# A mixture-of-experts layer on one core: a transposed wide form for experts over 128 tokens, longer weight pieces, and permuted features

## The chip, the cores and the metric

One program runs on one core of a Trainium2 chip. The metric is the device time of one execution in microseconds (us); lower is better. The core has TensorE (PE: matmuls, with weight loads shown apart as PEld), VectorE (DVE), ScalarE (ACT), GpSimd (POOL) and SyncE (SP, which only issues DMAs here), and 16 DMA engines behind the DMA queues.

## The reference, cut to what matters

The layer has a mixer (attention and a short convolution), a mixture of experts, and a gated per-layer embedding. The change touches the experts:

```
# 2048 tokens, D = 1024 features, hidden size FF = 512, 32 experts, 2 experts per token
xn = rmsnorm(h)                                # (2048, 1024) float32
group logits = xn @ w_group_router             # top group of 4
expert logits = xn @ w_expert_router           # top 2 of the 8 experts of that group
for every expert e, over the tokens routed to it:
    hidden = silu(x @ w_gate[e]) * (x @ w_up[e])    # (n, 1024) @ (1024, 512)
    y      = hidden @ w_down[e]                     # (n, 512) @ (512, 1024)
h += sum over a token's two experts of weight * y
```

With the inputs of the runs 16 of the 32 experts have more than 128 tokens (experts 0, 2, 8 to 11, 15 to 18, 20, 22, 25 to 27 and 31); the largest has 155.

## The kernel before, in words

**Precision by splitting.** Every float32 operand of a matmul is split into a high and a low part: ACT copies the tile to `uh` (the rounded value), DVE subtracts that to get `ul`. A product then takes three matmuls, `hi*hi`, `hi*lo` and `lo*hi`, added up in one PSUM bank; `mm3` issues them (L73, L74, L75, in the order uh·xh, ul·xh, uh·xl as the names of the trace have it).

**Weights.** Each expert has 12 units of 512 KB: four of `w_gate`, four of `w_up`, four of `w_down`. SP loads unit by unit into a ring of 12 raw slots (`load_unit`, `unit_loads`); `split_unit` turns a raw slot into a pair `uh`, `ul` in a ring of 10 (L65 on ACT, L66 on DVE); PE reads the pairs. `free()` in an expert's block splits the next unit into the pair just used up and issues the loads for which room is left. A partition's piece of a `w_gate` load is two rows of 2 KB, of a `w_up` load four rows of 1 KB, of a `w_down` load one row of 4 KB.

**Tokens.** POOL gathers the first 128 tokens of an expert into `xg0` (one token a partition) and, for an expert with more, up to 64 "others" into `xg1`; that second gather stands in an `If` of its own one expert ahead. PE transposes them (128x128 for the first, 64x64 for the others) and ACT and DVE split the results into `xh`, `xl` (features on partitions, 128 tokens) and `xs` (64 tokens, high and low side by side). What exceeds 192 tokens would go through another loop, `far_experts`; it has no work here.

**An expert's block.** The 32 experts are written out one after the other. Each is an `If` on its count: `block(e, True)` for over 128 tokens (called wide below), else `block(e, False)` (near). In both the tokens are the stationary operand and the weights move past them. Near: per unit of `w_gate` two times three matmuls of 512 columns, per unit of `w_up` four times three of 256, per unit of `w_down` two times three of 512. After the second and fourth `w_up` unit, DVE multiplies with the silu of the gate to get `u` (128 tokens x 256 hidden values, L1299), PE transposes it (L1306), ACT and DVE split it into `hh`, `hl`, which are the stationary operand of the `w_down` products. Wide does the same and, one unit later, the others: two matmuls for each weight piece (L1285 with `uh`, L1286 with `ul`) against a stationary tile with 64 high and 64 low columns; ACT copies the low half of the result and DVE adds it (`half`, L1250, L1251). PE's, ACT's and DVE's orders are the order of the code (`manual_schedule`).

The next expert's first tokens are transposed inside the block, after its down units 8 and 9 (L1229); the others' eight 64x64 transposes stand at the start of the wide block (L1356). After the last unit ACT copies the results to `y` and POOL stores them.

Of the kernel before, what the change touches and what calls it, by code (L numbers as in the profile page):

```python
# [20 lines left out]
S, D = 2048, 1024  # L21
# [11 lines left out]

R1 = E * 128
R2 = R1 + E * 64
FAR = 192
# [14 lines left out]
class Kernel:  # L51
# [689 lines left out]
    def ring(self, st):  # L741

        p = self.pool(st, "raws", 1, side="right")
        self.raws = [p.tile([128, D], F32, name=f"raw{i}") for i in range(NRAW)]
        p = self.pool(st, "ring", 1)
        self.units = [(p.tile([128, D], F32R, name=f"uh{i}"), p.tile([128, D], F32R, name=f"ul{i}"))
                      for i in range(NSPLIT)]
        self.rp = self.pool(st, "rt", 1)
        self.nload = self.nsplit = 0

    def load_unit(self, src):
        raw = self.raws[self.nload % NRAW]
        self.nload += 1
        self.nc.sync.dma_start(raw if len(src.shape) == 2 else raw.rearrange("p (k f) -> p k f", k=src.shape[1]), src)

    def split_unit(self, scale=None, pool=False, later=None):
# [3 lines left out]
        uh, ul = self.units[self.nsplit % NSPLIT]  # L760
        self.nsplit += 1
# [5 lines left out]
        return uh, ul  # L767

# [5 lines left out]
    def mix_out(self, st):  # L774
# [50 lines left out]
        nc.sync.dma_start(rwr[:, :, :NGR], a["w_group_router"][0].rearrange("(k p) e -> p k e", p=128))  # L825
        nc.sync.dma_start(rwr[:, :, NGR:], a["w_expert_router"][0].rearrange("(k p) e -> p k e", p=128))
# [72 lines left out]
        def route(t0, n):  # L899
# [90 lines left out]
            yield V.tensor_scalar(u1, e_, -64.0, float(R1 - 128), op0=OP.mult, op1=OP.add)  # L990
# [122 lines left out]
        for e in range(2):  # L1113
            self.gather(e, 0)
        self.gather(0, 1)
# [28 lines left out]
        for k in range(2):  # L1144
            self.trans(0, 4 * k, pst)

# [35 lines left out]
    def unit_loads(self, most=NRAW):  # L1182

        a = self.a
        stop = min(self.nload + most, self.nsplit + NRAW, UNITS + 4)
        while self.nload < stop:
            i, j = divmod(self.nload - 10, 12)
            k, u = divmod(j, 4)
            if self.nload >= UNITS:
# [4 lines left out]
            elif k == 0:  # L1194
                src = a["w_gate"][0, i, u * 256:u * 256 + 256].rearrange("(k p) f -> p k f", p=128)
            elif k == 1:
                f, r = divmod(u, 2)
                src = a["w_up"][0, i, r * 512:r * 512 + 512, f * 256:f * 256 + 256].rearrange("(k p) f -> p k f", p=128)
            else:
                src = a["w_down"][0, i, u * 128:u * 128 + 128]  # L1200
            self.load_unit(src)

    def expert_tiles(self):
# [4 lines left out]
        self.idx1 = cp.tile([64, E], I32, name="idx1")  # L1208
        self.xT = [self.xt_pair(cp, 0)]
        self.xg = [[cp.tile([n, D], F32, name=f"xg{r}{i}") for i in range(2)] for r, n in enumerate((128, 64))]  # L1210
# [4 lines left out]
    def xt_pair(self, p, i):  # L1215
        return [p.tile([128, KD, 128], F32R, name=f"{n}{i}") for n in ("xh", "xl")]
# [8 lines left out]
    def trans(self, e, kk, pst):  # L1225
        xh, xl = self.xT[e % 2]
# [3 lines left out]
        self.split(xh[:, kk:kk + 4], xl[:, kk:kk + 4], ps)  # L1230
# [6 lines left out]
    def experts(self, st):  # L1237
        tc, nc = self.tc, self.nc
        V, mm = nc.vector, nc.tensor.matmul
        self.xT.append(self.xt_pair(self.pool(self.est, "e_x1", 1), 1))  # L1240
# [3 lines left out]
        self.banks = [psm.tile([128, 512], F32, name=f"bank{i}") for i in range(6)]  # L1244

        def half(ps, n, out=None):

            lo = wk.tile([64, 512], F32, name="lo", bufs=1)
            r = wk.tile([64, 256], F32, name="sum", bufs=1) if out is None else out
            nc.scalar.activation(lo[:, :n], ps[64:128, :n], AF.Copy)  # L1250
            V.tensor_tensor(r[:, :n], ps[0:64, :n], lo[:, :n], op=OP.add)  # L1251
            return r

        def block(e, more):

            xh, xl = self.xT[e % 2]
            pg, pg1, pu, pu1 = self.banks[0], self.banks[1], self.banks[2::2], self.banks[3::2]
            ys, y1 = self.banks[2:4], self.banks[4:6]
            unit = lambda j: self.units[(10 + 12 * e + j) % NSPLIT]
            hh = wk.tile([128, 4, 128], F32R, name="hh", bufs=1)  # L1260
            hl = wk.tile([128, 4, 128], F32R, name="hl", bufs=1)
            if more:
                xs = wk.tile([128, KD, 2, 64], F32R, name="xs", bufs=1)
                hs = wk.tile([128, 4, 2, 64], F32R, name="hs", bufs=1)

            def free():

                self.next_unit()

            def prods(j, r):  # L1270

                uh, ul = unit(j)
                if j < 4:
                    n, ks, nk, out = 512, (2 * j, 2 * j + 1), KD, [(pg, pg1)[r]]
                elif j < 8:
                    f, i = divmod(j - 4, 2)
                    n, ks, nk, out = 256, range(4 * i, 4 * i + 4), KD, [(pu, pu1)[r][f]]
                else:
                    n, ks, nk, out = 512, (j - 8, j - 8), 4, (ys, y1)[r]
                for i, k in enumerate(ks):  # L1280
                    ps = out[i % len(out)][:, :n]
                    wh, wl = uh[:, i * n:i * n + n], ul[:, i * n:i * n + n]
                    if r:
                        s = xs[:, k] if j < 8 else hs[:, k]
                        mm(ps, s, wh, start=k == 0, stop=False)  # L1285
                        mm(ps, s, wl, start=False, stop=k == nk - 1)  # L1286
                    else:
                        s = (xh[:, k], xl[:, k]) if j < 8 else (hh[:, k], hl[:, k])
                        self.mm3(ps, [(*s, wh, wl)], start=k == 0, stop=k == nk - 1)

            def hidden(f, r):

                fs = slice(f * 256, f * 256 + 256)
                if r:
                    u = half(pu1[f], 256)[:, :256]
                    V.tensor_tensor(u, u, sl1[:, fs], op=OP.mult)
                else:
                    u = wk.tile([128, 256], F32, name="u", bufs=1)
                    V.tensor_tensor(u, pu[f][:, :256], sl[:, fs], op=OP.mult)  # L1299
                return u  # L1300

            def hidden_trans(f, r, u):
                n = 64 if r else 128
                ps = self.pst.tile([128, 4, 128], F32, name="tr")[:, :2, :n]
                for k in range(2):
                    nc.tensor.transpose(ps[:, k], u[:, k * 128:k * 128 + 128], self.ident[:n, :n])  # L1306
                K = slice(2 * f, 2 * f + 2)
                if r:
                    self.split(hs[:, K, 0], hs[:, K, 1], ps)
                else:  # L1310
                    self.split(hh[:, K], hl[:, K], ps)

            def store(r):
                y = wk.tile([128, D], F32, name="y", tag="h")
                for f in range(2):
                    fs = slice(f * 512, f * 512 + 512)
                    if r:
                        half(y1[f], 512, y[:64, fs])
                    else:
                        nc.scalar.activation(y[:, fs], ys[f], AF.Copy)  # L1320
                if r:
                    nc.gpsimd.dma_start(self.yd[R1 + e * 64:R1 + e * 64 + 64], y[:64])
                else:
                    nc.gpsimd.dma_start(self.yd[e * 128:e * 128 + 128], y)  # L1324

            U = {}

            def first(j):
                prods(j, 0)
                if j == 3:  # L1330
                    nc.scalar.activation(sl, pg, AF.Silu)
                if j in (5, 7):
                    U[j] = hidden((j - 5) // 2, 0)
                if j in (6, 8):
                    hidden_trans((j - 6) // 2, 0, U[j - 1])
                if j in (8, 9) and e + 1 < E:
                    self.trans(e + 1, 4 * (j - 8), self.pst)
                if j == 11:
                    store(0)

            def others(j):
                prods(j, 1)
                if j == 3:
                    half(pg1, 512, sl1)
                    nc.scalar.activation(sl1, sl1, AF.Silu)
                if j in (5, 7):
                    U[-j] = hidden((j - 5) // 2, 1)
                if j == 11:
                    store(1)

            sl = wk.tile([128, 512], F32, name="sil", bufs=1)
            if more:
                sl1 = wk.tile([64, 512], F32, name="sil1", bufs=1)
                ps = self.pst.tile([128, KD, 64], F32, name="tr")
                for k in range(KD):
# [403 lines left out]
```

## Time and profile before

| | |
|---|---|
| runs of the kernel | 2375.61 us median of 3 (2374.02 to 2383.3) |
| the profiled execution | 2378.32 us, span of its trace 2376.6 us |
| TensorE | 2262.7 us busy, 95% of the span, mean granted clock 0.988 |
| VectorE, ScalarE, GpSimd | 72%, 56%, 20% busy |
| before the experts | 0 to 1264.4 us of the span |
| the 32 experts | 1264.4 to 2134.0 us |
| after them | 2134.0 to 2376.6 us |

The durations below come from the profiled execution. A busy PE is not a PE at its peak: the printed duration of one matmul includes its fill and drain, which overlap the next; what a stream of matmuls costs is read from the distance between their starts.

### The profile page before, as it was taken

What the parts mean: (1) busy time and instruction counts of PE and PEld (TensorE: products, weight loads), DVE (VectorE), ACT (ScalarE), POOL (GpSimd) and SP (SyncE); (2) the same over time, 40 slices, a digit from 0 to 9 for tenths busy, and PEclk for the clock granted to TensorE, in tenths of its full rate; (3) what the DMA queues carried; (4) which work ended last, traced back from release to release, by engine and by line L of the source; (5) the groups of instructions that cost most, each with busy time, mean ns of one, the idle gap of its engine ahead of it and who ended that gap; (6) DMA issues with size and microseconds to landing.
All of it is one profiled execution on the core that took longest, in us unless ns stands there. A gap on an engine that the chain in (4) does not pass through costs nothing. (4 is left out here: it accounts for less than half of the span.)

```text
span 2376.6 us, 34881 instructions
## 1 busy us (share of the span) xinstructions
PE 2262.7 (95%) x12058; PEld 1869.0 (79%) x12058; DVE 1700.2 (72%) x3109; ACT 1341.3 (56%) x2407; POOL 481.8 (20%) x570
## 2 busy tenths in 40 slices
PE   7999999999999999999988999999999999999997
PEld 6888888888888888778866877787787777778775
DVE  5756666648888888866775777668667776766887
ACT  5334334328888888732236676667556666665443
POOL 0121212022333333401131000101001111003432
PEclk9999999999999999999999999999999999999999
DMA  7363635464556443566647899779777896873552
GB/s 226 100 224 95 223 94 180 110 197 128 134 129 130 90 90 78 133 207 203 205 151 239 293 331 320 230 229 360 230 235 268 288 323 227 290 253 131 173 194 96
DMA packets 297850, 465.68 MB, mean 196 GB/s; under 512 B 27609, under 2 KB 197634, under 8 KB 297602
## 3 DMA queue, kind: packets, MB, share of 16 engines
q1 hardware_dynamic: 253696, 333.43, 45.8%
q0 software_dynamic: 36384, 105.53, 13.6%
q10 hardware_dynamic: 7522, 23.61, 2.7%
q8 instruction: 133, 2.18, 0.4%
q14 instruction: 115, 0.94, 0.2%
HBM read 369.04 MB, written 97.62 MB: 196 GB/s over the span
## 5 line engine op out<-in xcount | busy, mean ns | idle before, releaser
L66 DVE TENSOR_TENSOR ul<-raw,uh 128x1024 fp32r<-128x1024 f32 x396 | 478.6, 1229 | 189.7 <-ACT uh L65 179.5
L65 ACT ACTIVATE uh<-raw 128x1024 fp32r<-128x1024 f32 x396 | 403.2, 1052 | 94.1 <-PE bank L1285 47.5
L73 PE MATMUL bank<-uh,xh 128*128 128x256 f32 (+1 forms) x768 | 252.8, 329 | 21.5 <-ACT uh L65 16.2
L75 PE MATMUL bank<-uh,xl 128*128 128x256 f32 (+1 forms) x768 | 248.3, 323 | 1.2 <-issue 1.2
L74 PE MATMUL bank<-ul,xh 128*128 128x256 f32 (+1 forms) x768 | 248.3, 323 | 1.2 <-issue 1.2
L66 DVE TENSOR_TENSOR pt<-tr,pt 128x512 fp32r<-128x512 f32 (+2 forms) x320 | 194.4, 609 | 60.5 <-ACT pt L65 56.7
L65 ACT ACTIVATE pt<-tr 128x512 fp32r<-128x512 f32 (+2 forms) x317 | 169.0, 534 | 74.3 <-PE tr L653 69.3
L73 PE MATMUL mm<-xh,wh 128*128 128x512 f32 x536 | 210.4, 393 | 0.0
L74 PE MATMUL mm<-xl,wh 128*128 128x512 f32 x536 | 210.2, 392 | 0.0
L75 PE MATMUL mm<-xh,wl 128*128 128x512 f32 x536 | 210.2, 392 | 0.0
L641 ACT ACTIVATE P<-s,mx 128x512 f32<-128x512 f32 (+2 forms) x320 | 199.2, 623 | 17.7 <-DVE mx L632 10.5
L664 PE MATMUL av<-pt,v 128*128 128x512 f32 (+3 forms) x640 | 204.0, 402 | 0.0
L632 DVE TENSOR_REDUCE mx<-s 128x1 f32<-128x512 f32 (+2 forms) x320 | 192.3, 602 | 8.6 <-PE s L629 4.1
L65 ACT ACTIVATE wh<-raw 128x1024 fp32r<-128x1024 f32 x68 | 72.0, 1060 | 216.5 <-PE mm L74 164.9
L73 PEld LDWEIGHTS bank<-uh,xh 128*128 128x128 f32 x768 | 146.7, 191 | 40.5 <-issue 26.7
L653 PE MATMUL tr<-ident,P 128*128 128x128 f32 x1088 | 172.8, 274 | 0.3 <-DVE pt L66 0.3
L75 PEld LDWEIGHTS bank<-uh,xl 128*128 128x128 f32 x768 | 146.6, 191 | 15.1 <-issue 3.1
L74 PEld LDWEIGHTS bank<-ul,xh 128*128 128x128 f32 x768 | 146.8, 191 | 12.7
L1324 POOL DMA_DIRECT2D yd<-y x32 | 18.2, 568 | 675.6 <-ACT y L1320 620.7
L66 DVE TENSOR_TENSOR xl<-tr,xh 128x512 fp32r<-128x512 f32 x160 | 106.1, 685 | 61.5 <-ACT xh L65 57.3
L653 PEld LDWEIGHTS tr<-ident,P 128*128 128x128 f32 x1088 | 128.7, 141 | 24.1 <-DVE pt L66 1.5
L66 DVE TENSOR_TENSOR wl<-raw,wh 128x1024 fp32r<-128x1024 f32 x68 | 82.9, 1220 | 83.2 <-ACT wh L65 81.9
(366 smaller groups left out, 5456.6 us busy)
## 6 DMA issues: line engine op xcount, KB each, us to landing
raw<-in_w_gate_dram SPq DMA_DIRECT2D x128, 512.0 KB, 4.8
raw<-in_w_up_dram SPq DMA_DIRECT2D x128, 512.0 KB, 5.7
raw<-in_w_down_dram SPq DMA_DIRECT2D x128, 512.0 KB, 6.1
raw<-in_w_in_dram SPq DMA_DIRECT2D x68, 512.0 KB, 3.9
yd<-y POOLq DMA_DIRECT2D x32, 512.0 KB, 6.5
xr<-in_x_dram SPq DMA_DIRECT2D x16, 512.0 KB, 6.7
kd<-stg POOLq DMA_DIRECT2D x16, 512.0 KB, 5.4
vd<-stg POOLq DMA_DIRECT2D x16, 512.0 KB, 5.2
```

Source lines behind the costliest of these rows:

```text
L65: nc.scalar.activation(hi, src, AF.Copy)
L66: f = lambda: (lo_eng or nc.vector).tensor_tensor(lo, src, hi.bitcast(F32), op=OP.subtract)
L73: mm(ps, ah, bh, start=(start and i == 0), stop=False)
L74: mm(ps, ah, bl, start=False, stop=False)
L75: mm(ps, al, bh, start=False, stop=(stop and i == n - 1))
L632: nc.vector.tensor_reduce(mx[:, c:c + 1], s, axis=AX.X, op=OP.max, negate=(g == 0))
L641: nc.scalar.activation(G["P"][qi][:, j * 512:j * 512 + s.shape[1]], s, AF.Exp, bias=nm, accum_out=G["rs"][:, qi, j:j + 1])
L653: nc.tensor.transpose(ps[:, jj], G["P"][qi][:, j * 128:j * 128 + 128], self.ident)
L664: mm(G["av"][:, q0:], heads[h]["v"][:, j], G["pt"][jq][:, hl, jj, q0:], start=(j == 0 and hl == 0), stop=(j == 4 * g + 3 and hl == 1))
L1324: nc.gpsimd.dma_start(self.yd[e * 128:e * 128 + 128], y)
```

## The change

**The wide form.** An expert may now have up to 160 tokens in this loop (`XT = 32` others instead of 64). One tile `xT` per expert holds, for each of the 8 feature blocks, 160 high and 160 low columns. In `wide` the weights become stationary for gate and up: a 128x128 chunk of `uh` meets all 320 columns, the same chunk of `ul` the 160 high ones. The hidden values come out transposed, so they need no transposes: ACT copies the 160 columns of `uh` x low, DVE adds them (`whole`), DVE multiplies, and ACT and DVE write the tile `H`, the stationary operand of the down products, which stay as they were (24 + 16 matmuls of 512 columns).

**The near form** keeps its matmuls. The two `hidden_trans` and the transposes of the next expert's tokens stand elsewhere, and eight 32x32-shaped transposes of the next expert's others are added in every block (`trans_others`). The gather of the others is issued for every expert, two ahead, without its `If`.

**The loads.** A `w_gate` piece is 4 KB contiguous a partition, and `w_up` comes in two DMAs of 1 MB with 8 KB a partition, each into two neighbouring raw slots; such a load needs both slots free. To match, feature `p*8 + k` rather than `k*128 + p` stands on partition `p` of block `k`: the rmsnorm writes its result permuted (a strided read and write), and the router weights are loaded in that order.

The core of the diff; of `near` and `wide`, which together replace `block`, the main lines of the new code stand without a sign:

```
+XT = 32
+FAR = 128 + XT
-FAR = 192
 def load_unit(self, src):
         raw = self.raws[self.nload % NRAW]
-        self.nload += 1
+        n = 1
+        if len(src.shape) == 3:
+            n = src.shape[1] // 2
+            if n == 2:
+                raw = self.pairs[self.nload % NRAW // 2].rearrange("p n d -> p (n d)")
+            raw = raw.rearrange("p (k f) -> p k f", k=2 * n)
+        self.nload += n
+        self.nc.sync.dma_start(raw, src)
 def unit_loads(self, most=NRAW):
+            if self.nsplit + NRAW < self.nload + {4: 3, 5: 2, 6: 2}.get(j, 1):
+                break
-                src = a["w_gate"][0, i, u * 256:u * 256 + 256].rearrange("(k p) f -> p k f", p=128)
+                src = a["w_gate"][0, i].rearrange("(p k) f -> p k f", p=128)[:, 2 * u:2 * u + 2]
-                src = a["w_up"][0, i, r * 512:r * 512 + 512, f * 256:f * 256 + 256].rearrange("(k p) f -> p k f", p=128)
+                src = a["w_up"][0, i].rearrange("(p k) f -> p k f", p=128)[:, 2 * u:2 * u + 4]
 def norm(t, ss):
-            V.scalar_tensor_tensor(xns[t], hs.pop(t), r, gbc, op0=OP.mult, op1=OP.mult)
+            order = lambda x: x.rearrange("p (q k) -> p k q", k=KD)
+            V.scalar_tensor_tensor(xns[t].rearrange("p (k q) -> p k q", k=KD), order(hs.pop(t)), r, order(gbc),
+                                   op0=OP.mult, op1=OP.mult)
+def near(e):
+            for j in range(7):
+                first(j)
+                if j == 3:
+                    nc.scalar.activation(sl[:, :512], pg, AF.Silu)
+                if j == 5:
+                    hidden(0)
+                free()
+            first(7, (0, 1))
+            hidden_trans(0)
+            first(7, (2, 3))
+            hidden(1)
+            next_trans(e, 0)
+            next_trans(e, 1)
+            products(e, 8, H, ys, (0,))
+            hidden_trans(1)
+            products(e, 8, H, ys, (1,))
+            next_trans(e, 2)
+def wide(e):
+                for b, ps in enumerate(out):
+                    for i in range(nk):
+                        k = k0 + i
+                        for t in range(2):
+                            c = (i * nt + 2 * b + t) * 128
                            cs = slice(c, c + 128)
+                            mm(ps[:, t, :2 * FAR], uh[:, cs], X[:, k], start=k == 0, stop=False)
+                            mm(ps[:, t, :FAR], ul[:, cs], X[:, k, 0], start=False, stop=k == KD - 1)
+            def whole(out, ps):
+                nc.scalar.activation(lo, ps[:, :, FAR:2 * FAR], AF.Copy)
+                V.tensor_tensor(out, ps[:, :, :FAR], lo, op=OP.add)
...
+            for j in range(8):
+                first(j)
+                if j < 3:
+                    next_trans(e, j)
+                if j == 3:
+                    for b in range(2):
+                        whole(sl[:, 2 * b:2 * b + 2], gate[b])
+                    nc.scalar.activation(sl, sl, AF.Silu)
+                if j in (5, 7):
+                    hidden((j - 5) // 2)
+                free()
+            for j in (8, 9):
+                products(e, j, H, ys)
+                others(j)
+                free()
 for e in range(E):
             if e + 2 < E:
-                self.gather(e + 2, 0)
-            if e + 1 < E:
-                with tc.If(self.counts[e + 1] > 128):
-                    self.gather(e + 1, 1)
+                for r in range(2):
+                    self.gather(e + 2, r)
```

PE at the second `w_gate` unit of the wide block of expert 0, before (`bank` is a PSUM bank, `xs` the others' stationary tile; the last number is partitions x columns):

```order
L73 MATMUL bank_13781<-uh_10182,xh_12714 128x512
L74 MATMUL bank_13781<-ul_10183,xh_12714 128x512
L75 MATMUL bank_13781<-uh_10182,xl_12715 128x512
...
L1285 MATMUL bank_13782<-uh_10180,xs 128x512
L1286 MATMUL bank_13782<-ul_10181,xs 128x512
```

and at the first chunks of its first `w_gate` unit in the changed kernel:

```order
L1390 MATMUL bank_13781<-xT_12704,uh_10172 128x320
L1391 MATMUL bank_13781<-xT_12704,ul_10173 128x160
...
L1390 MATMUL bank_13782<-xT_12704,uh_10172 128x320
L1391 MATMUL bank_13782<-xT_12704,ul_10173 128x160
```

The weights have become the loaded operand, and ten matmuls of 512 columns for a unit and its others have become eight pairs of 320 and 160.

PE from the first `w_down` unit of a near block on, before:

```order
L73 MATMUL bank_13784<-uh_10196,hh 128x512
L74 MATMUL bank_13784<-ul_10197,hh 128x512
L75 MATMUL bank_13784<-uh_10196,hl 128x512
L1306 MATMUL tr<-ident,u 128x128 x2
L1229 MATMUL tr<-ident,xg_12717 128x128 x4
L73 MATMUL bank_13783<-uh_10198,hh 128x512
```

and around the same unit in the changed kernel (`mm3` has lines L74 to L76 there, `hidden_trans` L1338):

```order
L76 MATMUL bank_13783<-uh_10186,xT_12704 128x256
L1256 MATMUL tr<-ident,xg_12706 128x128 x8
L74 MATMUL bank_13782<-uh_10188,H 128x512
L75 MATMUL bank_13782<-ul_10189,H 128x512
L76 MATMUL bank_13782<-uh_10188,H 128x512
L1338 MATMUL bank_13781<-ident,u 128x128 x2
L74 MATMUL bank_13782<-uh_10188,H 128x512
L75 MATMUL bank_13782<-ul_10189,H 128x512
L76 MATMUL bank_13782<-uh_10188,H 128x512
L1264 MATMUL tr<-ident,xg_12708 128x32 x8
```

Between the last `w_up` matmul and the transposes of the second half of `u` (L1306, now L1338) there stood six matmuls, now eight transposes of the next expert's tokens and three matmuls; the others' transposes (L1264) are new.

SP's loads in one block, before:

```order
L754 DMA raw_10171<-in_w_down_dram 128x1024
...
L754 DMA raw_10175<-in_w_gate_dram 128x2x512
...
L754 DMA raw_10167<-in_w_up_dram 128x4x256
```

and in the changed kernel:

```order
L763 DMA raw_10167<-in_w_down_dram 128x1024 x2
L763 DMA raw_10168<-in_w_gate_dram 128x1024 x2
L763 DMA raw_10163<-in_w_gate_dram 128x1024 x2
L763 DMA raw_10164<-in_w_up_dram 128x2048
L763 DMA raw_10165<-in_w_up_dram 128x2048
```

A block issued four loads of each kind; now it issues two for `w_up`, of twice the size.

## Rows read from the trace of the kernel before

**Rows 1.** Windows by stage: length, busy time (count) PE PEld DVE ACT POOL, clock, DMA share, GB/s.

```profile
1264.40:2134.00 869.60, 811.65 (x4657) 684.03 (x4656) 617.78 (x732) 562.27 (x750) 91.71 (x91) 0.99 0.81 275
```

**Rows 2.** The same view, two runs of four wide blocks each.

```profile
1461.30:1593.50 132.20, 125.14 (x729) 105.97 (x729) 86.73 (x111) 79.31 (x112) 14.69 (x15) 1.00 0.71 232
1655.30:1787.40 132.10, 125.13 (x729) 105.87 (x728) 86.88 (x111) 79.34 (x112) 15.15 (x15) 1.00 0.73 235
```

**Rows 3.** The same view, five and three near blocks in a row.

```profile
1352.50:1461.30 108.80, 97.96 (x550) 81.79 (x549) 85.17 (x93) 76.62 (x97) 10.11 (x11) 0.97 0.97 338
1593.50:1655.30 61.80, 57.24 (x334) 47.99 (x333) 51.39 (x57) 46.24 (x59) 8.01 (x7) 1.00 1.00 355
```

**Rows 4.** Timeline of PE in a wide block: start, printed duration, instruction.

```profile
1330.25 0.39 PE L1285 MATMUL bank<-uh,xs 128*128 128x512 f32 x1
1330.48 0.40 PE L1286 MATMUL bank<-ul,xs 128*128 128x512 f32 x1
...
1331.18 0.28 PE L73 MATMUL bank<-uh,xh 128*128 128x256 f32 x1
1331.30 0.27 PE L74 MATMUL bank<-ul,xh 128*128 128x256 f32 x1
```

**Rows 5.** Timeline of PE in the attention: 128-column matmuls, each with new weights.

```profile
532.20 0.22 PE L627 MATMUL s<-k,q 96*128 96x128 f32 x1
532.26 0.28 PE L628 MATMUL s<-k,q 96*128 96x128 f32 x1
532.38 0.27 PE L629 MATMUL s<-k,q 96*128 96x128 f32 x1
532.49 0.23 PE L631 MATMUL s<-maskb,identb 128*128 128x128 bf16 x1
```

**Rows 6.** The same view, the weight loads of these matmuls.

```profile
532.21 0.19 PEld L628 LDWEIGHTS s<-k,q 96*128 96x128 f32 x1
532.32 0.19 PEld L629 LDWEIGHTS s<-k,q 96*128 96x128 f32 x1
```

**Rows 7.** Timeline of PE, transposes and waits of wide blocks; brackets: idle before, releaser.

```profile
1341.25 0.60 PE L1229 MATMUL tr<-ident,xg 128*128 128x128 f32 x4
1510.30 0.44 PE L1306 MATMUL tr<-ident,u 128*128 128x128 f32 x2 [0.86 <-DVE u L1299]
1516.72 0.33 PE L1306 MATMUL tr<-ident,sum 64*128 64x64 f32 x2 [0.58 <-DVE hl L66]
1527.37 0.68 PE L1356 MATMUL tr<-ident,xg 64*128 64x64 f32 x8 [0.36 <-PE bank L1286]
```

**Rows 8.** The same view, waits of PE in and behind a near block.

```profile
1363.16 0.44 PE L1306 MATMUL tr<-ident,u 128*128 128x128 f32 x2 [0.61 <-DVE u L1299]
1366.67 0.44 PE L1306 MATMUL tr<-ident,u 128*128 128x128 f32 x2 [0.24 <-DVE u L1299]
1374.87 0.47 PE L73 MATMUL bank<-uh,xh 128*128 128x512 f32 x1 [2.69 <-ACT uh L65]
```

**Rows 9.** Branches of the block's If on PE's queue, 1367 to 1376, 1345 to 1352.5.

```profile
L1394 PEldq COMPARE_BRANCH  x1: 5694/5694/5694, 1369.0 to 1369.0; - x1
L1394 PEldq COMPARE_BRANCH  x2: 301/1444/2587, 1348.4 to 1349.4; - x2
```

**Rows 10.** Groups of DVE and ACT in the experts: count, busy, mean ns, idle before.

```profile
L66 DVE TENSOR_TENSOR ul<-raw,uh 128x1024 fp32r<-128x1024 f32 x378 | 454.8, 1222 | 181.4 <-ACT uh L65 171.4 <-DMA raw<-in_w_down_dram 4.2 <-DMA raw<-in_w_up_dram 2.2
L1299 DVE TENSOR_TENSOR u<-bank,sil 128x256 f32<-128x256 f32 x64 | 26.7, 417 | 0.0
L65 ACT ACTIVATE hh<-tr 128x256 fp32r<-128x256 f32 x64 | 24.6, 385 | 71.5 <-PE tr L1306 48.1 <-issue 23.4
```

**Rows 11.** DMA queues in the experts: packets, MB, share of 16 engines.

```profile
q1 hardware_dynamic: 117476, 200.92, 68.9%
q0 software_dynamic: 11264, 36.23, 11.2%
```

**Rows 12.** The rmsnorm ahead of the experts, by line: min/median/max ns.

```profile
L1036 DVE SCALAR_TENSOR_TENSOR xn<-h,rms_r,gbc x16: 1283/1285/1287, 1017.9 to 1220.1; 128x1024 f32<-128x1024 f32 x16
```

More of the change, by code (lines that the diff above doesn't have):

```diff
@@ L760, in split_unit @@
         uh, ul = self.units[self.nsplit % NSPLIT]
+        i, j = divmod(self.nsplit - 10, 12)
+        if 0 <= i < E and 4 <= j < 8:
+            f, r = divmod(j - 4, 2)
+            pair = self.pairs[(self.nsplit - j + 4 + 2 * r) % NRAW // 2].rearrange("p n (k c) -> p (n k) c", k=2)
+            raw = pair[:, :, f * 256:f * 256 + 256]
+            uh, ul = (u.rearrange("p (k c) -> p k c", k=4) for u in (uh, ul))
         self.nsplit += 1
@@ L1243, in experts @@
         psm = self.pool(st, "e_psm", 1, space=PSUM)
[L1244 to L1272, printed above, removed]
+        banks = [psm.tile([128, 2, 512], F32, name=f"bank{i}") for i in range(3)]
@@ new lines, in experts, with tiles, next_trans, products @@
+        free = self.next_unit
+        def tiles():
+            return (wk.tile([128, 4, 2 * FAR], F32R, name="H", bufs=1),
+                    wk.tile([128, 4, FAR], F32, name="sil", bufs=1))
+        def next_trans(e, i):
+            if e + 1 < E:
+                if i < 2:
+                    self.trans(e + 1, 4 * i, self.pst)
+                else:
+                    self.trans_others(e + 1, self.pst)
+        def products(e, j, H, ys, parts=(0, 1)):
+            uh, ul = self.unit(e, j)
+            k = j - 8
+            for f in parts:
+                fs = slice(f * 512, f * 512 + 512)
+                self.mm3(ys[:, f], [(H[:, k, :128], H[:, k, FAR + XT:], uh[:, fs], ul[:, fs])], start=k == 0, stop=k == 3)
@@ new lines, in store, with first @@
+        def store(e, ys):
+            y = wk.tile([128, D], F32, name="y", tag="h")
+            for f in range(2):
+                nc.scalar.activation(y[:, f * 512:f * 512 + 512], ys[:, f], AF.Copy)
+            nc.gpsimd.dma_start(self.yd[e * 128:e * 128 + 128], y)
+        def near(e):
+            X = self.xT[e % 2]
+            H, sl = tiles()
+            sl = sl.rearrange("p a b -> p (a b)")
+            pg, tr, pu, ys = banks[0][:, 0], banks[0][:, 1], (banks[1][:, 0], banks[2][:, 0]), banks[1]
+            U = []
+            def first(j, ks=None):
+                uh, ul = self.unit(e, j)
@@ L1273, in prods @@
                 if j < 4:
[L1274 to L1275 removed]
+                    n, k0, nk, ps = 512, 2 * j, 2, pg
+                else:
                     f, i = divmod(j - 4, 2)
[L1277 to L1289 removed]
@@ L1313, in store, with hidden @@
-            def store(r):
-                y = wk.tile([128, D], F32, name="y", tag="h")
+                    n, k0, nk, ps = 256, 4 * i, 4, pu[f][:, :256]
+                for i in ks or range(nk):
+                    k, ns = k0 + i, slice(i * n, i * n + n)
+                    self.mm3(ps, [(X[:, k, 0, :128], X[:, k, 1, :128], uh[:, ns], ul[:, ns])], start=k == 0, stop=k == KD - 1)
+            def hidden(f):
+                u = wk.tile([128, 256], F32, name="u", bufs=2)
+                V.tensor_tensor(u, pu[f][:, :256], sl[:, f * 256:f * 256 + 256], op=OP.mult)
+                U.append(u)
@@ new lines, in hidden_trans @@
+            def hidden_trans(f):
+                ps = tr[:, :256].rearrange("p (k q) -> p k q", k=2)
+                for k in range(2):
+                    nc.tensor.transpose(ps[:, k], U[f][:, k * 128:k * 128 + 128], self.ident)
+                K = slice(2 * f, 2 * f + 2)
+                self.split(H[:, K, :128], H[:, K, FAR + XT:], ps)
+            free()
[7 more added lines that the diff above has]
+                free()
@@ new lines, in near @@
+            first(7, (0, 1))
[8 more added lines that the diff above has]
+            next_trans(e, 2)
+            free()
+            free()
+            products(e, 9, H, ys)
+            free()
+            products(e, 10, H, ys)
+            products(e, 11, H, ys)
+            store(e, ys)
@@ L1328, in first @@
[L1328 to L1355, printed above, removed]
-                    nc.tensor.transpose(ps[:, k], self.xg[1][e % 2][:, k * 128:k * 128 + 128], self.ident[:64, :64])
-                self.split(xs[:, :, 0], xs[:, :, 1], ps)
+                    mm(y1[:2 * XT, f], H[:, k, 128:FAR + XT], uh[:, fs], start=k == 0, stop=False)
@@ new lines, in wide @@
+            for j in (8, 9):
+                products(e, j, H, ys)
+                others(j)
+                free()
+            products(e, 10, H, ys)
+            products(e, 11, H, ys)
+            store(e, ys)
+            others(10)
+            others(11)
+            y = wk.tile([XT, D], F32, name="y1", bufs=1)
+            lo = wk.tile([XT, D], F32, name="lo1", bufs=1)
+            for f in range(2):
+                fs = slice(f * 512, f * 512 + 512)
+                nc.scalar.activation(lo[:, fs], y1[XT:2 * XT, f], AF.Copy)
+                V.tensor_tensor(y[:, fs], y1[:XT, f], lo[:, fs], op=OP.add)
@@ L1388, in experts @@
             if e + 2 < E:
-                self.gather(e + 2, 0)
-            if e + 1 < E:
-                with tc.If(self.counts[e + 1] > 128):
-                    self.gather(e + 1, 1)
+                for r in range(2):
+                    self.gather(e + 2, r)
             n = self.nsplit, self.nload
             with tc.If(self.counts[e] > 128) as c:
-                block(e, True)
+                wide(e)
             self.nsplit, self.nload = n
             with c.Else():
-                block(e, False)
+                near(e)
     def far_experts(self, st):
```

119 lines of the change are left out of this document (51 added, 68 removed).

## The prediction
> **What bounds the kernel now.** I read the windows by stage first, since the change touches one stage: the 32 experts take 869.6 of 2376.6 us, with PE 811.65 us busy at a clock of 0.99, DVE 617.78, ACT 562.27 and the DMA engines 81% of the time [rows 1]. PE is the first suspect, but the mean hides two kinds of block, so the second view is the same window over runs of equal blocks. Eight wide blocks take 132.20 + 132.10 us, 33.04 each, with PE busy 125 of 132, DVE only 87, and the DMA engines at 0.71 to 0.73 [rows 2]: these are PE's. Eight near blocks take 108.80 + 61.80 us, 21.3 each, PE idle for 10% and 7% of it, and the DMA engines at 0.97 and 1.00 [rows 3]: there the transfers are at their limit while PE has little slack. The third view is the timeline of PE, for the price of each matmul and for the waits inside a block; the fourth the branches and the DMA queues.
>
> The prices: in a stream, four matmuls of 512 columns lie between the starts 1330.25 and 1331.18, so 0.233 us each, and one of 256 takes 0.12 [rows 4]. That is 0.455 and 0.47 ns a column; I use 0.46. A 128x128 transpose costs 0.11 (0.44 for four, the printed 0.60 holds a drain), eight 64x64 ones (0.68 - 0.22)/7 = 0.066 each [rows 7].
>
> **Wide: what goes.** Gate and up now take 24 + 16 matmuls of 512 columns (w_gate: 8 feature blocks, for each 3 matmuls for the first tokens and 2 for the others) and 48 + 32 of 256 (w_up, in two halves). 40 x 0.233 + 80 x 0.12 is 9.3 + 9.6 = 18.9 us. After, there are 64 pairs (8 feature blocks, 4 chunks of 128 hidden values, for w_gate and w_up). A pair is 320 + 160 = 480 columns, 0.22 us at 0.46 ns: 64 x 0.2225 = 14.2 us. **Minus 4.7.** The columns fall from 41.0 to 30.7 thousand.
>
> This price isn't shown by a row, since no matmul of 320 or 160 columns exists. From below it is bounded by the columns. From above by the weight loads: every matmul now brings new weights, and 128-column matmuls with new weights start 0.12 and 0.11 us apart (532.26, 532.38, 532.49) although their columns take 0.06 [rows 5]; the loads themselves start 0.11 apart [rows 6]. Two loads a pair fit into 0.22. If the load for the next 320 could begin only once the 160 has begun and had to be whole before the 320 starts, a pair would cost 0.147 + 0.11 = 0.2575, 16.5 us in all, minus 2.4 instead of minus 4.7. I take 0.2225: the matmul at 532.26 starts 0.05 after its load has begun at 532.21, so a matmul follows the load's head, and the 0.075 of the 160 covers that.
>
> The opposite would be that a load never lies beside a matmul: 0.147 + 0.11 + 0.075 + 0.11 = 0.44 a pair, 28 us in all, and a wide block 14 us longer than forecast. The load at 532.21 speaks against it: it begins 0.01 after the start of a matmul printed with 0.22 us, and 256-column matmuls with alternating weights keep 0.12, which leaves no room for a bare 0.11 [rows 4 to 6].
>
> The Trainium skill (TensorE: Matmul & The Clock Gate, Part 3, "The mechanism") lists under what overlaps that a weight load overlaps matmuls in flight only when the row group differs; all loads here use the full height, so by that line the kernel would be slower. The same section also lets a load into a background buffer be pulled ahead, and this kernel's trace agrees with that one.
>
> Down products are unchanged (40 x 0.233 = 9.3 us). Transposes: four of `u` at 0.11, four of the others' `sum` and the eight 64x64 of `xg1` at some 0.066 to 0.11 go, 0.44 + 0.44 + 0.53 = 1.4 us; eight with 32 columns come. The bounds of these are 0 and 0.53 (the 64x64 ones); I take 0.3. **Minus 1.1.** Waits in the block: 0.86 on `u`, 0.58 on `hl` and 0.36 at the start [rows 7], each for a round trip through DVE or ACT that the new form either hasn't or covers. In its place stands one new chain: after the last `w_up` matmul of a half, ACT copies, DVE adds and multiplies, ACT copies, DVE subtracts twice. With rows of 385 (ACT) and 417 ns (DVE) for 256 columns [rows 10] and 320 here, I estimate about 2.5 us. For the first half it lies under the 16 pairs of the two units behind it, 3.6 us. For the second half, the first two down units, 20 matmuls or 4.7 us, need only the first half of H and cover it. Without the cover each half would cost up to 2.5. So I take 0.1 for waits: **minus 1.7**. I add **0.4** for the start of a block (the first bank is emptied late by the block before) and the higher load on ACT and DVE. Together 4.7 + 1.1 + 1.7 - 0.4 = **minus 7.1 a wide block**, 33.0 to 25.9.
>
> Do the others keep up at 25.9? DVE needs 86.8/4 = 21.7 us a wide block now [rows 2], of which 12 x 1.222 = 14.7 are the weights [rows 10]; the rest is of equal size after (fewer, longer operations), so 22: covered by 4 us. ACT is below that. DMA: the queues use 68.9% + 11.2% of 869.6 us, 697 us or 21.8 a block [rows 11]; the bytes stay. That is 84% of 25.9.
>
> **Near.** The matmuls stay. The eight new transposes cost 0.3 (bounds 0 and 0.53). The waits on `u`, 0.61 and 0.24 [rows 8], are moved behind six more matmuls of 256 columns (0.72) and behind eight transposes less three matmuls; I take 0.5 of the 0.85 as gone. The If around the gather of the others goes, a branch less on each queue, 0.2. **Minus 0.4**, between 0 and minus 0.85. What is left behind a near block is its branch: it kept PE's queue for 5.69 us at 1369.0, so that the next matmul came 2.69 late, and 2.59 at most behind a wide one [rows 9, 8]. That branch jumps over the code of the other form, and the longer of the two stands where the DMA engines are full. I cost it as unchanged, which is the weak spot: below are its bounds.
>
> **Loads and norm.** A `w_up` piece grows from 1 to 8 KB, a `w_gate` piece from 2 to 4. No row prices that alone. Queue q1 moves 200.92 MB in 599 us of engine time, 335 GB/s; q0, with its 4 KB rows, 36.23 MB in 97 us, 372 GB/s [rows 11]. Between no gain and q1 at q0's rate lie 0 and 59 us of engine time, not of path: wide blocks hide it all, near ones may get some back. The later start of a pair's load (it needs two free slots) costs nothing while 12 slots lie ahead: the wait of DVE for loads is 4.2 + 2.2 us in the whole stage [rows 10]. The strided norm costs at most its own duration again, 1.3 us each [rows 12], and only the last is on the path: 0 to 1.3, taken as 0.5.
>
> **The sum.** 16 x (-7.1 - 0.4) = -120 us, +0.5: 2378.3 to 2258. The profiled execution stands 2.7 us above the median of the runs shown; the median is forecast at **2256 us**, minus 5.0%. Changes within 0.5%, 12 us, can hardly be told from none here.
>
> **The rivals.**
> 1. The weight loads set the pace, a pair is 0.2575. For it: the 0.11 between loads [rows 6] is half a pair, with no slack. Against it: the start of the matmul 0.05 after its load. 16 x 2.24 = 36 us more: 2292. Chance 0.12.
> 2. The fuller DMA engines slow the branches. Wide blocks rise from 0.72 to 0.84 of the engines or more, and bigger pieces hold an engine longer ahead of the fetched code. By the list of experts a near block follows a wide one 7 times and a near one 9 times. If the 7 branches go from 2.6 to 5.3 us, about what the near one took [rows 9], and the 9 get 1.5 longer, that is 19 + 13 = 32 us: 2288. Chance 0.14.
> 3. The bigger pieces relieve the queue, and of a near block's 2.7 us over its PE work (21.3 against 48 x 0.233 + 48 x 0.12 + 12 x 0.11 + 0.3 = 18.6) another 1.9 goes: 30 us less, 2226. For it: the 59 us of engine time above. Against it: PE waits there behind a branch, not for a weight transfer [rows 8, 9]. Chance 0.09.
> 4. The other side: each weight load stands bare between two matmuls, a pair takes 0.44 and a wide block 14 us longer, 224 us in all: 2480. The kernel is no faster once a pair costs more than 0.2225 + 120/(16 x 64) = 0.34. Against it: rows 5 and 6 as read above. Chance 0.03. The line of the Trainium skill cited above (TensorE: Matmul & The Clock Gate, Part 3, "The mechanism") amounts to this.
> 5. No change: the wide form saves PE's time but a wide block goes on waiting for its weights, so that it keeps 33 us. At 21.8 us of engine time a block the transfers would have to run at two thirds of their pace in rows 3. Chance 0.02, 2376.
>
> The forecast itself has 0.60, with a range of its own of 2240 to 2274 (1 us a wide block, about its allowances). **Range 2222 to 2298**: it takes in rivals 1 to 3 nearly whole. Faster by over 0.5%: 0.95; same: 0.02; slower: 0.03.
>
> **What would show it.** In the trace after: pairs starting 0.22 apart (right), 0.26 (rival 1) or 0.44 (rival 4); wide runs at 26 us a block, with PE over 95% busy; no wait of PE over 0.3 us at the hidden chains; near runs at 20.9 a block; branches of the block's If of 2.6 to 5.7 us as before (longer is rival 2, shorter rival 3), and a DMA share of 0.85 to 0.93 in the stage. The forecast falls if a wide block waits for weights, which the windows would show as DVE and PE idle together with the DMA share at 1.

## The result, and the profile after

The changed kernel takes 2298.77 us (median of 4 runs, 2295.84 to 2300.98) against 2378.68 us for the one before (4 runs): a ratio of 0.966 with an interval of 0.964 to 0.969, so 3.4% faster. The forecast was 2256, and the time lies 0.8 us above the upper end of its range. The profiled execution took 2295.84 us, 82.5 less than the one before. The windows by stage and over the same runs of blocks (columns as in [rows 1]):

```profile
1259.90:2050.80 790.90, 758.22 (x4784) 659.25 (x4784) 600.80 (x731) 545.21 (x733) 111.62 (x106) 0.99 0.83 300
1445.90:1560.80 114.90, 110.67 (x738) 98.57 (x736) 82.66 (x108) 74.49 (x105) 13.83 (x16) 1.00 0.76 268
1622.40:1737.70 115.30, 110.66 (x738) 98.55 (x736) 83.15 (x108) 74.47 (x105) 14.74 (x16) 1.00 0.77 269
1338.50:1445.90 107.40, 99.21 (x581) 83.25 (x580) 85.49 (x97) 78.28 (x100) 19.41 (x16) 0.97 0.92 341
1560.80:1622.40 61.60, 58.48 (x348) 49.06 (x349) 51.17 (x59) 46.26 (x59) 11.08 (x9) 1.00 0.95 351
```

The experts fell from 869.6 to 790.9 us [rows 1], 78.7 of the 82.5. Eight wide blocks take 114.9 + 115.3 us, 28.8 each, after 33.04 [rows 2]: 4.3 gained where 7.1 was forecast. Eight near blocks take 107.4 + 61.6, 21.1 each, after 21.3 [rows 3]: 0.2 where 0.4 was forecast. These are half of the blocks; by the same view over all 16 of a kind, the wide ones fell from 529.5 to 455.7 us, 4.6 each, and the near ones from 340.1 to 335.3, 0.3 each. So the missing time is in the wide blocks, and PE is busy there 96% of the time: it is hardly waiting, its work is dearer than forecast. The timeline of PE in a wide block shows the pairs:

```profile
1473.87 0.24 PE L1391 MATMUL bank<-xT,ul 128*128 128x160 f32 x1
1473.94 0.35 PE L1390 MATMUL bank<-xT,uh 128*128 128x320 f32 x1
1474.12 0.24 PE L1391 MATMUL bank<-xT,ul 128*128 128x160 f32 x1
1474.20 0.35 PE L1390 MATMUL bank<-xT,uh 128*128 128x320 f32 x1
...
1475.94 0.41 PE L1390 MATMUL bank<-xT,uh 128*128 128x320 f32 x1 [1.06 <-ACT lo L1443]
```

and the weight loads of the same place:

```profile
1473.87 0.19 PEld L1390 LDWEIGHTS bank<-xT,uh 128*128 128x128 f32 x1
1473.98 0.19 PEld L1391 LDWEIGHTS bank<-xT,ul 128*128 128x128 f32 x1
1474.13 0.19 PEld L1390 LDWEIGHTS bank<-xT,uh 128*128 128x128 f32 x1
1474.24 0.19 PEld L1391 LDWEIGHTS bank<-xT,ul 128*128 128x128 f32 x1
```

A pair lasts 0.26 (1473.94 to 1474.20), not 0.2225. The loads suggest why: the load for the 320 columns starts as the 160-column matmul starts (1473.87), the next load 0.11 later (1473.98), the one after that 0.15 later (1474.13), which is the length of 320 columns. Read so, the 160-column matmul, 0.075 by its columns, holds its place for 0.11, until the load behind it is in; the experiments with other widths test this. The printed starts of the matmuls (0.07 after their load, then 0.18 on) lie ahead of that.

The largest waits of PE in the whole stage, and one smaller that is needed below (us in total, times, longest; L74 to L76 and L1338 stand in near blocks, L1390 in wide ones):

```profile
PE bank L74 <- issue: 10.2, 8, 2.2
PE bank L1390 <- ACT lo L1443: 8.5, 8, 1.1
PE bank L1338 <- DVE u L1332: 4.6, 4, 1.6
PE bank L75 <- issue: 4.5, 1, 4.5
PE bank L76 <- issue: 1.3, 1, 1.3
PE bank L1390 <- ACT y L1306: 1.2, 7, 0.2
```

Nothing of the hidden chains of the wide form stands there, so the down units cover them as forecast. One wait is new: eight times a wide block behind a wide one stands for about 1.06 us at its fifth pair, the first that writes the bank of the block before's results.

### The profile page after: what moved, and what is told of

It is laid out like the page before. It is cut to its first block, busy times and chain, and to the rows that moved or that the text cites. A ratio compares the mean times of both kernels' runs of the same rounds, so it can differ in the third digit from the quotient of the medians.

```text
span 2294.1 us, 34784 instructions
## 1 busy us (share of the span) xinstructions
PE 2205.3 (96%) x12186; PEld 1844.3 (80%) x12186; DVE 1698.9 (74%) x3109; ACT 1324.8 (58%) x2391; POOL 503.7 (22%) x584
## 5 line engine op out<-in xcount | busy, mean ns | idle before, releaser
L67 DVE TENSOR_TENSOR ul<-raw,uh 128x1024 fp32r<-128x1024 f32 x396 | 469.1, 1227 | 118.9 <-ACT uh L66 117.0
L66 ACT ACTIVATE uh<-raw 128x1024 fp32r<-128x1024 f32 x396 | 397.8, 1051 | 33.4 <-PE bank L76 11.2
L1390 PE MATMUL bank<-xT,uh 128*128 128x320 f32 x1024 | 275.9, 351 | 10.8 <-ACT lo L1443 8.5
L1391 PE MATMUL bank<-xT,ul 128*128 128x160 f32 x1024 | 243.4, 238 | 0.0
L74 PE MATMUL mm<-xh,wh 128*128 128x512 f32 x536 | 210.5, 393 | 0.0
L76 PE MATMUL mm<-xh,wl 128*128 128x512 f32 x536 | 210.2, 392 | 0.0
L1390 PEld LDWEIGHTS bank<-xT,uh 128*128 128x128 f32 x1024 | 193.4, 189 | 15.5 <-ACT lo L1443 10.0
L1391 PEld LDWEIGHTS bank<-xT,ul 128*128 128x128 f32 x1024 | 196.8, 192 | 0.7
L67 DVE TENSOR_TENSOR wl<-raw,wh 128x1024 fp32r<-128x1024 f32 x68 | 82.9, 1220 | 82.8 <-ACT wh L66 82.5
L74 PE MATMUL bank<-uh,xT 128*128 128x256 f32 (+1 forms) x384 | 126.3, 329 | 11.4 <-issue 10.2
L75 PE MATMUL bank<-ul,xT 128*128 128x256 f32 (+1 forms) x384 | 123.9, 323 | 4.5 <-issue 4.5
L76 PE MATMUL bank<-uh,xT 128*128 128x256 f32 (+1 forms) x384 | 124.5, 324 | 1.3 <-issue 1.3
```

The lines of the kernel that those rows point to most:

```text
L66: nc.scalar.activation(hi, src, AF.Copy)
L67: f = lambda: (lo_eng or nc.vector).tensor_tensor(lo, src, hi.bitcast(F32), op=OP.subtract)
L74: mm(ps, ah, bh, start=(start and i == 0), stop=False)
L75: mm(ps, ah, bl, start=False, stop=False)
L76: mm(ps, al, bh, start=False, stop=(stop and i == n - 1))
L1390: mm(ps[:, t, :2 * FAR], uh[:, cs], X[:, k], start=k == 0, stop=False)
```

## The experiments

Each is the changed kernel with the edit shown, compared with the kernel before on the same chip.

**The changed kernel again.** 2298.36 us (5 runs), ratio 0.966 [0.964, 0.968]. The runs with 240 columns, the old loads and the pieces of 4 KB were on its chip, the others on two more.

> The changed kernel as it is, for comparison on the same chip: 2299 us within 0.3% by every theory.

**240 columns in the second matmul.**

```
-mm(ps[:, t, :FAR], ul[:, cs], X[:, k, 0], start=False, stop=k == KD - 1)
+mm(ps[:, t, :240], ul[:, cs], X[:, k].rearrange("p a b -> p (a b)")[:, :240],
+   start=False, stop=k == KD - 1)
```

> The second matmul of each pair moves 240 columns instead of 160 (the low half's first 80 too; the products that it adds belong to the result). Theory A, weight loads set the pace: a matmul lasts the longer of its columns and 0.11 us, so 160 columns cost 0.11 and 240 cost 0.11 as well; a pair stays at 0.257 and the time at 2299 (within 6). Theory B, a pair costs its columns and a fixed 0.035 on top: 80 columns more at 0.46 ns are 0.037 a pair, 64 x 16 pairs, 2299 + 38 = 2337.

Measured: 2302.59 us, ratio 0.9675 [0.965, 0.970]. Half as many columns again cost 4 us, within the spread of its runs (2295.75 to 2305.45), where 38 were due if columns count. The timeline of PE:

```profile
1479.88 0.31 PE L1390 MATMUL bank<-xT,uh 128*128 128x320 f32 x1
1480.03 0.27 PE L1391 MATMUL bank<-xT,ul 128*128 128x240 f32 x1
1480.13 0.31 PE L1390 MATMUL bank<-xT,uh 128*128 128x320 f32 x1
```

The pair is 0.25 to 0.26 again, now split 0.15 and 0.10 to 0.11 as the columns have it: 240 columns (0.11 us at 0.46 ns) just fill the load.

**320 columns in the second matmul** (the same edit with 320).

> The second matmul of each pair moves all 320 columns. Theory A (a matmul lasts the longer of its columns and the 0.11 us of the next load): 0.147 + 0.147 = 0.294 a pair against 0.257, 64 x 16 x 0.037 = 38 us more, 2337. If columns beyond 160 were free as such, 2299; with a fixed cost of 0.035 on top of the columns, 0.33 a pair and 2373.

Measured: 2339.86 us, ratio 0.983 [0.981, 0.985]; 41 more than the changed kernel, where theory A has 38. Above the length of a load, columns count in full, without a fixed cost on top.

**64 columns in the second matmul** (the same with 64).

> The second matmul of each pair moves 64 columns instead of 160; it leaves out the product of the weights' low half with the other 96 tokens. Theory A (a matmul lasts at least the 0.11 us of a weight load): a pair stays at 0.257, 2299 within 6. If columns set the price, 96 x 0.46 ns x 1024 = 45 us less, 2254; the forecast's own price would give that.

Measured: 2297.33 us, ratio 0.9645 [0.9625, 0.966]. 96 columns fewer save nothing:

```profile
1480.09 0.40 PE L1390 MATMUL bank<-xT,uh 128*128 128x320 f32 x1
1480.32 0.19 PE L1391 MATMUL bank<-xT,ul 128*128 128x64 f32 x1
1480.35 0.39 PE L1390 MATMUL bank<-xT,uh 128*128 128x320 f32 x1
```

The printed starts now stand 0.23 and 0.03 apart, and the pair is still 0.26. With 64, 160, 240 and 320 columns the times are 2297, 2298, 2303 and 2340: flat up to the load's length, then a slope.

**The order 320, 320, 160, 160.**

```
-for t in range(2):
-    mm(... uh[:, cs], X[:, k] ...); mm(... ul[:, cs], X[:, k, 0] ...)
+for t in range(2):
+    mm(... uh[:, cs[t]], X[:, k] ...)
+for t in range(2):
+    mm(... ul[:, cs[t]], X[:, k, 0] ...)
```

> The same matmuls in the order 320, 320, 160, 160 instead of 320, 160, 320, 160. Theory A: two of 0.147 and two of 0.11, the same 0.515 for the four, 2299 within 6; in the timeline the second 160 starts 0.11 after the first. If the lost 0.035 belonged to the change from a short to a long matmul, it would come once instead of twice in four: 18 us less, 2281.

Measured: 2296.30 us, ratio 0.965 [0.963, 0.967], not to be told from the changed kernel. The loss doesn't hang on the change from short to long; it comes with every short matmul.

**The old loads under the new forms.** `w_gate` and `w_up` sources, `split_unit`, the rmsnorm and the router weights as in the kernel before; for instance

```
-src = a["w_up"][0, i].rearrange("(p k) f -> p k f", p=128)[:, 2 * u:2 * u + 4]
+f, r = divmod(u, 2)
+src = a["w_up"][0, i, r * 512:r * 512 + 512, f * 256:f * 256 + 256].rearrange("(k p) f -> p k f", p=128)
```

> The changed kernel with the loads, the order of features and the rmsnorm of before (w_gate in pieces of 2 KB, w_up in pieces of 1 KB, twelve loads an expert); the wide and near forms are the new ones. If the loads brought nothing, 2299 (within 6). If they relieve the near blocks, whose DMA share was 0.97 to 1.00 before and 0.90 to 0.95 after, the near blocks lose up to 0.7 us each again and some wide ones that follow them: 2305 to 2320. If fuller engines in the shorter wide blocks need the longer pieces, more: over 2320.

Measured: 2300.12 us, ratio 0.9665 [0.965, 0.9685]: the longer pieces and the permuted features are worth nothing that can be told. Their effect stays in the engines. The DMA queue of the weights, with the old loads and in the changed kernel:

```profile
q1 hardware_dynamic: 117254, 199.57, 73.4%
```

```profile
q1 hardware_dynamic: 46405, 200.97, 70.8%
```

That is 73.4% of a window of 790 us with the old loads and 70.8% of 790.9 with the new: some 20 us less engine time, in packets two and a half times fewer, and none of it shows in the kernel's time.

**Pieces of 4 KB for w_up.**

```
-        self.nc.sync.dma_start(raw, src)
+        if n == 2:
+            for h in range(2):
+                self.nc.sync.dma_start(raw[:, 2 * h:2 * h + 2], src[:, 2 * h:2 * h + 2])
```

> w_up in four loads of 512 KB with pieces of 4 KB instead of two of 1 MB with 8 KB. If an 8 KB piece is the better one, 2299 or up to 10 us more. If 8 KB pieces hold an engine up (the new kernel's queue moved 359 GB/s while busy, with w_down's and w_gate's 4 KB pieces in it), 2285 to 2297, from the near blocks.

Measured: 2299.49 us, ratio 0.967 [0.965, 0.969], the same. The size of the pieces isn't what this kernel waits for.

**The others' tail first.**

```
-products(e, 10, H, ys); products(e, 11, H, ys); store(e, ys)
 others(10); others(11)
 (the copies of y1 and its store)
+products(e, 10, H, ys); products(e, 11, H, ys); store(e, ys)
```

> At the end of a wide block the others' last two down units and their copies come before the first tokens' last two units, so that the last work of ACT in the block is the copy of ys and not the others' second copy. If the wait of 1.06 us that a wide block behind a wide one has at its fifth pair is for ACT's end in the block before, it falls to 0.2 to 0.4 in the 8 such blocks, 8 x 0.7 = 5 us, and something in the blocks ahead of near ones: 2290 to 2296. If it is for something else, 2299.

Measured: 2290.61 us, ratio 0.963 [0.961, 0.964], 8 less than the changed kernel. The waits of PE:

```profile
PE bank L1390 <- ACT y L1306: 2.7, 15, 0.2
```

The row of 8.5 us on ACT's `lo` is gone and that on its `y` grows from 1.2 to 2.7, at most 0.2 us a block: 7.0 of the 8 us. In the code the fifth pair writes the bank of `ys`, which the copies `y` read; `lo` reads another, that of `y1`. In the changed kernel's trace these two reads lie so:

```profile
1472.06 1.09 ACT L1306 ACTIVATE y<-bank 128x512 f32<-128x512 f32 x2 [1.39 <-PE bank L76]
1475.30 0.59 ACT L1443 ACTIVATE lo<-bank 32x512 f32<-32x512 f32 x1 [0.74 <-DVE y L1444]
```

The bank's own reader had ended at 1473.15, `lo` at 1475.89, and PE went on at 1475.94. So in both orders a block's first write to the old results' bank waited for the last work of ACT in the block before. What makes it wait for that isn't shown.

**That and the grouped order together** (both edits).

> The others' tail first and the order 320, 320, 160, 160 together: if the first is worth 8 us and the second nothing, 2291; if the 2 us of the second are real, 2288.

Measured: 2289.38 us, ratio 0.961 [0.960, 0.963]. It is the fastest version run; its interval lies below the changed kernel's, but not below that of the others' tail alone.

**The near block's transposes where they were.**

```
-first(7, (0, 1)); hidden_trans(0); first(7, (2, 3)); hidden(1)
-next_trans(e, 0); next_trans(e, 1)
-products(e, 8, H, ys, (0,)); hidden_trans(1); products(e, 8, H, ys, (1,))
-next_trans(e, 2)
+(hidden_trans(0) behind first(6)); first(7); hidden(1)
+products(e, 8, H, ys); hidden_trans(1); next_trans(e, 0)
+products(e, 9, H, ys); next_trans(e, 1); next_trans(e, 2)
...
```

This is the order of before, but not quite its near block: the transposes of `u` still write a bank of the changed kernel (`bank<-ident,u`), where those of before wrote a `tr` buffer [rows 8].

> The near block with its transposes where they stood before: those of u behind the next unit, those of the next expert's tokens behind the down units 8 and 9, with the others' behind the latter. The forecast's step: the moved transposes save 0.5 us of waits a near block, so 16 x 0.5 = 8 us more, 2307. If what a near block waits for is its branch alone, so that PE's saved waits are only spent there, 2299.

Measured: 2318.59 us, ratio 0.9745 [0.972, 0.977], 20 more than the changed kernel, over twice the 8 expected. The waits of PE:

```profile
PE bank L1338 <- DVE u L1332: 15.2, 29, 2.4
PE bank L1388 <- DVE y L1442: 12.2, 8, 1.5
```

and the same near runs as above, by windows:

```profile
1343.20:1451.90 108.70, 99.70 (x581) 83.08 (x581) 85.68 (x97) 77.67 (x100) 20.23 (x16) 0.98 0.93 338
1568.40:1633.30 64.90, 60.00 (x348) 50.47 (x349) 51.35 (x59) 45.64 (x59) 12.46 (x9) 0.97 0.93 334
```

These 8 near blocks take 0.6 us more each ((108.7 + 64.9 - 107.4 - 61.6) / 8), but the other 8 take more than that. The sums of the same view over the stretches of all 16 near blocks, in the changed kernel and with the old order:

```profile
sum 335.31, PE 315.51 PEld 264.68 DVE 274.02 ACT 248.14 POOL 60.60; mean PE 45.07 PEld 37.81 DVE 39.15 ACT 35.45 POOL 8.66
sum 349.64, PE 321.35 PEld 270.71 DVE 275.46 ACT 245.88 POOL 61.37; mean PE 45.91 PEld 38.67 DVE 39.35 ACT 35.13 POOL 8.77
```

That is 14.3 us, 0.9 a block: 8.5 of waits, and 5.8 in which PE is busy longer with the same matmuls, with a granted clock of 0.93 to 0.96 in three stretches (experts 21, 23 with 24, 28 to 30) that had 0.97 to 1.00. The wait on `u` is 10.6 us longer in all. Another 3.7 is in the wait at the fifth pair of wide blocks, which now ends with DVE's `y` and lasts 12.2 in the place of 8.5; why it changes its releaser isn't shown. Together that is 18 of the 20 us.

**The near form as the If's first branch.**

```
-with tc.If(self.counts[e] > 128) as c:
-    wide(e)
+with tc.If(self.counts[e] < 129) as c:
+    near(e)
 with c.Else():
-    near(e)
+    wide(e)
```

> The changed kernel with the near form as the If's first branch and the wide one behind it. If a near block's lost 2.4 us are the jump over the wide code ahead of it, a near block behind a wide one has no jump left and those behind a near one still have one at the end of the block before; wide ones behind near ones get it instead: near blocks 0.5 to 1.5 us shorter, wide ones behind near ones as much longer, in sum 2290 to 2305. If the near blocks wait for transfers whatever jumps there are, they stay at 21.0 and nothing changes, 2299.

Measured: 2352.10 us, ratio 0.988 [0.986, 0.989]: 53 us more, with the same work and far outside the expectation. A wide block behind a near one now has two jumps ahead of it, over the wide code at the end of one near block and over the near code of its own expert. On PE's queue, from 1452 to 1466:

```profile
L1453 PEldq COMPARE_BRANCH  x2: 5060/5210/5361, 1453.4 to 1458.9; - x2
```

and the first matmul behind them:

```profile
1464.46 0.60 PE L1390 MATMUL bank<-xT,uh 128*128 128x320 f32 x1 [6.63 <-issue]
```

Two branches of over 5 us one behind the other outlast what PE has queued, and it stands for 6.63. In the changed kernel a near block and the wide one behind it lie one after the other in the code, with no far jump between. The waits of PE over the stage (1264.4 to 2106.6) have

```profile
PE bank L1390 <- issue: 39.5, 7, 8.3
PE bank L1390 <- ACT uh L66: 5.1, 1, 5.1
PE bank L1391 <- issue: 4.4, 1, 4.4
```

at wide blocks, where the changed kernel has no such row: 49 us. At near blocks the waits on issue fall from 16.0 us (10.2 + 4.5 + 1.3) to 4.7. The stage by windows, and the 4 us behind the wait of 6.63:

```profile
1264.40:2106.60 842.20, 771.35 (x4784) 673.21 (x4784) 601.46 (x731) 541.56 (x730) 107.64 (x105) 0.96 0.78 280
1464.40:1468.40 4.00, 3.94 (x17) 3.97 (x18) 0.00 (x0) 0.00 (x0) 0.02 (x1) 0.50 1.02 418
1465.00 0.55 PE L1390 MATMUL bank<-xT,uh 128*128 128x320 f32 x1
1465.47 0.55 PE L1390 MATMUL bank<-xT,uh 128*128 128x320 f32 x1
```

The stage takes 51.3 us more than the changed kernel's. PE is idle 38.2 us longer (842.20 - 771.35 against 790.90 - 758.22), and it is busy 13.1 us longer with the same matmuls. The second part goes with the clock: when PE went on after the 6.63 us, the granted clock was 0.50, the lower of its two levels (1.2 of 2.4 GHz), and a pair took 0.47 instead of 0.26; over the stage the mean is 0.96 against 0.99.

The changed kernel has two branches ahead of a near block behind a wide one as well, for instance

```profile
L1453 PEldq COMPARE_BRANCH  x2: 298/2272/4245, 1555.6 to 1556.3; - x2
```

In its seven such places the first takes 0.3 to 0.4 us and only the second 2.7 to 4.7. With the If turned round, both take 4.5 to 6.4 in five of the seven places ahead of a wide block behind a near one. Why isn't settled.

## Why the prediction was right or wrong

**The pair's price failed, and it is nearly the whole miss.** The step read "a matmul follows the load's head, and the 0.075 of the 160 covers that". It took the printed start of a matmul, 0.05 us behind the start of its load [rows 5, 6], for the time from which its columns run. But the same rows had the loads 0.11 apart, and that is what counts: a matmul holds its place for its columns or for the next one's load, whichever is longer, 0.147 + 0.11 = 0.2575 a pair. The four widths of the second matmul and the grouped order agree with that and with none of the other prices tried. That was the bound from above and rival 1, with its 36 us and 0.12 of the chance. It also means that the step "two loads a pair fit into 0.22" was the wrong test: the loads fit on the mean, but the load for the 320 columns isn't drawn ahead under the longer matmul of the pair before; in the rows above it begins only as the 160 begins.

The Trainium skill (TensorE: Matmul & The Clock Gate, "LDWEIGHTS (loading the stationary operand)") gives a load of 128 columns 107 ns by its formula, which agrees with the 0.11 here. The line of the Trainium skill on row groups that the prediction weighed (TensorE: Matmul & The Clock Gate, Part 3, "The mechanism") does not hold here, since a pair takes 0.26 and not the 0.44 of loads that lie beside no matmul.

**The transposes were mis-sized.** The eight new ones were taken at 0.3 us, with 0.53 as bound from the 64x64 ones of before. They are printed just like those, 0.68 [rows 7]:

```profile
1453.40 0.68 PE L1264 MATMUL tr<-ident,xg 32*128 32x32 f32 x8
```

So the bound is the better price: 0.2 us too little in each of 32 blocks, 6 us. No run changes these transposes alone.

**The waits of the wide block were right in sum.** The old ones are gone and the new hidden chain is covered. The 0.4 us allowed for the start of a block is, as measured, 8.5 us in 8 blocks, near the 6.4 that 16 allowances make. That the sums are near is luck: the wait is 1.06 in the eight blocks behind a wide one and 0.2 in the seven behind a near one, and its end, ACT's copies for the others at the end of the block before, was not named.

**Near blocks** gained 0.2 us by the windows, 0.3 over all 16, for a forecast of 0.4; with 0.2 more for the transposes that agrees. The 0.5 of waits that the moved transposes were to save is near the 10.6 us, 0.7 a block, by which the wait on `u` grew when they were put back. The whole cost of putting them back, 0.9 a near block, is more, but it includes a lower clock and was measured in a near block that isn't quite that of before.

**Loads and branches.** The forecast that longer pieces save engine time and none on the path is borne out by the old loads and by the 4 KB pieces; rival 3 has nothing for it, nor has rival 2: the branches of the block's If reach up to 6.0 us on PE's queue, after 6.4 before, and the DMA share of the stage is 0.83, a little under the 0.85 to 0.93 given:

```profile
L1453 PEldq COMPARE_BRANCH  x48: 65/305/6049, 1259.6 to 2046.5; - x48
```

That their cost stays unchanged fits this change; that they matter was shown by turning the If round.

The two wrong terms, 36 and 6 us, take the forecast from 2258 to 2300 for the profiled execution, which took 2295.84. By blocks it comes out the same: over all 16 of a kind the wide blocks gained 39.8 us less than forecast (73.8 for 16 x 7.1), the near ones 1.6 less (4.8 for 16 x 0.4).

## What to carry to other kernels

When each matmul brings new weights, price it as the longer of its columns and one weight load (0.46 ns a column, 0.11 us a load here, at a granted clock of 1.00), matmul by matmul and not as a mean over a pair; read the load's pace from the distance between loads, not from how soon a matmul is printed behind its load. In a form that makes weights stationary, a matmul with fewer columns than a load's length (240 here) pays for the load all the same, so count the short partner too; the form still gained here, with 160. At the border of two branches of an If, look at what the last work of each engine in a block is, since the next block's first write to a bank waited for that here and not for the bank's own reader; and try both orders of the branches, which were 53 us apart here. When an edit makes PE stand, look at the granted clock behind the wait before pricing the rest.

## What the runs showed that was not expected

Columns from 64 to 240 in the second matmul of a pair cost the same within 6 us. Turning the branches of the If round costs 53 us, of which 13 are matmuls at a lower granted clock behind the waits. With the old order of its transposes the near block takes 20 us of the gain of 80 away, twice the 10.6 that its wait on `u` grows by, and the length of the weights' pieces, from 1 KB to 8 KB, makes no difference that can be told.
